# Joint and up projection of an encoder layer: sum tiles of the last token tile, a third raw-weight place, and the order of passes and Gelu behind the evictions

## The chip, the cores and the metric

The kernel runs on one core of a Trainium2 chip. The metric is the device time of one execution in microseconds. Five engines work side by side, each through its own queue in order: TensorE (PE: matmuls and transposes), VectorE (DVE), ScalarE (ACT), GpSimd (POOL), and SyncE (SP), which here only issues DMA transfers. An instruction starts when it is at the head of its queue and the semaphores it waits for have come.

## The reference

One layer of a post-norm encoder over 1024 tokens of width 1024, in float32. Three sub-layers, each `h = layer_norm(alpha*h + f(h))`: a token mixer (mLSTM and neighbourhood attention), cross-attention into 256 memory tokens, and a gated feed-forward part. What follows concerns the border between the second and the third, and the third's first half:

```
def conv_ffn(x, w_up, b_up, w_dw, b_dw, w_down, b_down):
    h = x @ w_up + b_up
    h = lax.conv_general_dilated(h, w_dw[:, None, :], ...width 3, depthwise...) + b_dw
    g, u = jnp.split(h, 2, axis=-1)
    y = jax.nn.gelu(g, approximate=False) * u
    return y @ w_down + b_down
```

The hidden width is 2816, so `w_up` has 5632 columns: 22 blocks of 128 gate columns and 22 of 128 up columns.

## The kernel before

**Numbers.** A float32 operand is held as two float16 parts, a high part and the rest. A product of two such operands is three matmuls (`mm3`, L224 to L226: high by high, high by rest, rest by high). A split takes one ACT pass for the high part (L203) and one DVE pass for the rest (L204). Weights are first scaled by a power of two found from their largest absolute value.

**Units.** The up projection is done in 22 units (`Units`, L1507), one for each block of gate columns with its block of up columns. A unit is a 2 by 2 block product done with seven products in place of eight: A11·B11, A12·B21, S1·T1, S2·T2, S3·T3, S4·B22 and A22·T4. A is the unit's weight, B the tokens; S1 to S4 are sums of weight blocks, T1 to T4 sums of token blocks. Each product is 4 slices times 3 matmuls of 128 by 512, so a unit has 84 matmuls.

A unit `v` goes through these stages:

- `load` (L1515): one DMA of 1 MB into a raw place. Units 0 and 1 use `two0` and `two1`; later ones rotate over the two places of the tile `ur`.
- `bound` (L1522): ACT takes absolute values and their sum over the raw tile (L1524), DVE casts the result to `am` (L1525).
- `scale` (L1530): PE turns `am` round through a small matmul (`mx`, L182), DVE makes the scale `us` from it (L183, L174 to L176, L1533).
- `sums` (L1543): POOL makes S1 to S4 from the raw tile (L1547 to L1550) into two places called `wraw`.
- `split_A` and `split_S`: ACT L203 and DVE L204, three pieces each, into the home of `v % 4` (`unitYh`, `unitA` with `whi` and `wlo`, `unitYl`, or `whi` and `wlo`). The first piece reads the raw tile, the other two the sums.
- the seven products, into three PSUM banks X, Z and W.
- `take` (L1706): the evictions. On ACT are `m1` (L1709, after A11·B11), `u2` (L1713, after S2·T2), `u3` (L1715, after S3·T3) and `C21` (L1719, after A22·T4). On DVE are `C11` (L1711), `C22` (L1717) and `C12` (L1721).
- `post` (L1685 and around): the convolution of width 3 for gate and up part (ACT L1683, DVE L1684 and L1685 each), then Gelu on ACT (L1689), a multiply on DVE (L1690), the store of `y` (L1691) and a pass of absolute values on ACT (L1692).

The unit loop also holds a survey of the down weights (`survey_down`): a 512 KB load into `sv0` or `sv1`, and a pass of absolute values on ACT (L1728).

**The joint.** Token tiles come out of cross-attention one by one (`out_d`: residual, L1480, then the layer norm, L237 to L252). `to_B` (L1377) transposes a tile on PE (tile `tp`, L1381), evicts it with weight and bias of the norm (ACT L1284 for six of eight slices, DVE L1286 for two), and, for tiles with an odd number, makes T1 to T4 (DVE L1414, L1415, L1418, L1422) and splits them and B22 (`pair`: ACT L1411, DVE L1412). The sums T1 to T4 of a tile stand in the units' `wraw` places, except for the last two tiles: the last but one, here r6, uses `ysum`, and the last, r7, uses three tiles called `spare`, which share the places `vec0`, `vec1`, `vec2` with the surveys' `sv0` and `sv1`. Units 0 and 1 have their A11·B11 and A12·B21 beside this, and wait with S1·T1 for r7's T1.

**Who sets the order.** The program is written in the order of the listing, but the order in which each engine issues is set by a scheduler of the language, which lays the instructions out on a timeline of its own; `tc.issue_after(x)` makes an instruction stand behind `x` in the issue order. A tile's place is taken again when all readers of the one before are done (`reuse_waits="tile"`).

## Time and profile before

| what | value |
|---|---|
| three timed runs | 1477.83, 1480.55 and 1480.89 us, median 1480.55 us |
| the profiled execution, time | 1481.55 us |
| its span in the profile | 1479.8 us |
| mean granted TensorE clock | 0.993 |
| PE busy | 1435.1 us (97%) |
| DVE busy | 1034.1 us (70%) |
| ACT busy | 821.5 us (56%) |
| POOL busy | 553.5 us (37%) |

Times in the trace count from the start of the span. The profiled execution's own time is 1.75 us more than its span. The joint lies at about 820 to 850 us, the unit loop ends at about 1200 us, and behind it come the down projection and the last norm. Groups of instructions are named by engine and line; a row of a timeline gives the start, the duration, the engine, the line, output and inputs, and in brackets how long the engine stood idle before it and what ended that.

### The profile page before, as it was taken

The page shows a single profiled execution, that of the slowest core. Times are in us where ns is not written, and L with a number is a line of the kernel's source. Part 1 is how long each engine was busy: PE and PEld are TensorE (multiplying, and loading weights), DVE is VectorE, ACT ScalarE, POOL GpSimd, SP SyncE. Part 2 cuts the span into 40 slices and gives each one's busy share as a digit, 9 for nine tenths or more (in the row PEclk, how much of TensorE's full clock was granted, in tenths as well). Part 3 has the DMA queues.
Part 4 walks back from the last instruction along what each step waited for, and adds up shares of the span by engine and source line. Part 5 has one row for each costly group of instructions (what it writes and reads, how often), then busy time and mean ns, then how long its engine had stood idle before and what let it go on. Part 6 is the DMA issues. An engine that isn't in the chain of part 4 may idle for free. (4 is left out here: it accounts for less than half of the span.)

```text
span 1479.8 us, 21506 instructions
## 1 busy us (share of the span) xinstructions
PE 1435.1 (97%) x7996; PEld 844.2 (57%) x7996; DVE 1034.1 (70%) x1950; ACT 821.5 (56%) x1385; POOL 553.5 (37%) x440
## 2 busy tenths in 40 slices
PE   8999899999999999999999899999999999999998
PEld 6998776456766777774444444444444444444445
DVE  7867866535777778589658878787888888707424
ACT  5765465565563576424455777777777767403001
POOL 4452356502334766055114153343444400300543
PEclk9999999999999999999999999999999999999999
DMA  8845654214654644643343333233322437603121
GB/s 302 318 180 198 184 190 153 84 50 129 159 147 152 206 142 141 256 148 72 86 100 86 116 143 128 114 114 128 114 114 113 144 142 242 228 28 110 47 71 58
DMA packets 116383, 208.61 MB, mean 141 GB/s; under 512 B 40627, under 2 KB 69555, under 8 KB 112950
## 3 DMA queue, kind: packets, MB, share of 16 engines
q1 hardware_dynamic: 115984, 206.47, 42.0%
q8 instruction: 63, 1.03, 0.3%
q0 software_dynamic: 144, 0.49, 0.2%
q14 instruction: 42, 0.34, 0.1%
q10 hardware_dynamic: 150, 0.27, 0.0%
HBM read 154.15 MB, written 45.15 MB: 135 GB/s over the span
## 5 line engine op out<-in xcount | busy, mean ns | idle before, releaser
L1547 POOL TENSOR_TENSOR wraw<-ur 128x512 f32<-128x512 f32 x20 | 42.5, 2125 | 213.6 <-issue 193.0
L225 PE MATMUL dn<-wlo,yp 128*128 128x512 f16 (+1 forms) x284 | 105.1, 370 | 0.0
L224 PE MATMUL dn<-whi,yp 128*128 128x512 f16 (+1 forms) x284 | 104.9, 370 | 0.0
L226 PE MATMUL dn<-whi,yp 128*128 128x512 f16 (+1 forms) x284 | 104.4, 370 | 0.0
L1684 DVE SCALAR_TENSOR_TENSOR cbuf<-C,wdw,cbuf 128x1024 f32<-128x1024 f32 x44 | 71.4, 1623 | 30.8 <-ACT cbuf L1683 30.4
L225 PEld LDWEIGHTS <-whi 128*128 128x128 f16 x540 | 52.8, 98 | 58.0 <-issue 5.9
L226 PEld LDWEIGHTS <-wlo 128*128 128x128 f16 x540 | 52.8, 98 | 56.7 <-DVE wlo L204 1.3
L224 PEld LDWEIGHTS <-whi 128*128 128x128 f16 x540 | 52.8, 98 | 54.7 <-issue 1.7
L204 DVE SCALAR_TENSOR_TENSOR wlo<-wraw,us,whi 128x1024 f16<-128x1024 f32 (+1 forms) x48 | 62.8, 1325 | 21.3 <-ACT whi L203 21.3
L242 POOL TENSOR_TENSOR lnrs<-lnrs,mhalf 128x1 f32<-128x1 f32 x32 | 23.5, 735 | 127.4 <-DVE lnrs L241 90.2
L1685 DVE SCALAR_TENSOR_TENSOR cbuf<-C,wdw,cbuf 128x1024 f32<-128x1024 f32 x44 | 69.8, 1587 | 1.1
L1683 ACT ACTIVATE cbuf<-C,bdw,wdw 128x1024 f32<-128x1024 f32 x44 | 54.4, 1235 | 17.8 <-DVE C L1721 17.2
L1524 ACT ACTIVATE junk<-ur 128x2048 bf16<-128x2048 f32 x20 | 38.2, 1912 | 40.1 <-DMA ur<-in_w_up_dram 40.1
L203 ACT ACTIVATE whi<-wraw,us 128x1024 f16<-128x1024 f32 (+1 forms) x48 | 51.1, 1102 | 16.0 <-DVE us L176 15.8
L225 PEld LDWEIGHTS <-yp 128*128 128x128 f16 x370 | 36.2, 98 | 39.9
L224 PEld LDWEIGHTS <-yp 128*128 128x128 f16 x370 | 36.2, 98 | 39.8
L226 PEld LDWEIGHTS <-yp 128*128 128x128 f16 x370 | 36.2, 98 | 39.7
L224 PE MATMUL tk<-whi,Bo 128*128 128x256 f16 (+1 forms) x192 | 52.6, 274 | 2.9 <-DVE stage L204 2.9
L224 PE MATMUL tk<-whi,Be 128*128 128x256 f16 (+1 forms) x192 | 52.6, 274 | 0.9 <-DVE stage L204 0.8
L225 PE MATMUL tk<-wlo,Be 128*128 128x256 f16 (+1 forms) x192 | 52.4, 274 | 0.8 <-DVE wlo L204 0.8
L226 PE MATMUL tk<-whi,Bo 128*128 128x256 f16 (+1 forms) x192 | 52.5, 274 | 0.0
L226 PE MATMUL tk<-whi,Be 128*128 128x256 f16 (+1 forms) x192 | 52.5, 274 | 0.0
(555 smaller groups left out, 4802.2 us busy)
## 6 DMA issues: line engine op xcount, KB each, us to landing
ur<-in_w_up_dram SPq DMA_DIRECT2D x20, 1024.0 KB
sv<-in_w_down_dram SPq DMA_DIRECT2D x22, 512.0 KB
y<-cbuf SPq DMA_DIRECT2D x22, 512.0 KB
ur<-y SPq DMA_DIRECT2D x11, 1024.0 KB
wraw<-in_w_down_dram SPq DMA_DIRECT2D x22, 512.0 KB
r<-h SPq DMA_DIRECT2D x11, 512.0 KB
wraw<-in_w_tok_dram SPq DMA_DIRECT2D x10, 512.0 KB
wr<-in_w_xk_dram SPq DMA_DIRECT2D x8, 512.0 KB
```

Source lines behind the costliest of these rows:

```text
L203: A.activation(hi, src, AF.Copy, scale=s)
L204: return V.scalar_tensor_tensor(lo, src, s, hi, op0=OP.mult, op1=OP.subtract)
L224: T.matmul(ps, lh, rh, start=first, stop=False, skip_group_check=skip)
L225: T.matmul(ps, lh, rl, start=False, stop=False, skip_group_check=skip)
L226: return T.matmul(ps, ll, rh, start=False, stop=last, skip_group_check=skip)
L242: G.tensor_tensor(rs[:, 0:1], rs[:, 0:1], mhalf[:, 0:1], OP.pow)
L1524: A.activation(junk, self.raw[v], AF.Abs, accum_out=l1)
L1547: G.tensor_tensor(S1, A21, A22, OP.add)
L1683: A.activation(c, C[:, 1:SEQ + 1], AF.Identity, scale=wdw[:, 1, j:j + 1], bias=bdw[:, j:j + 1])
L1684: V.scalar_tensor_tensor(c, C[:, 0:SEQ], wdw[:, 0, j:j + 1], c, op0=OP.mult, op1=OP.add)
L1685: V.scalar_tensor_tensor(c, C[:, 2:SEQ + 2], wdw[:, 2, j:j + 1], c, op0=OP.mult, op1=OP.add)
```

## The change

Line numbers of the new kernel are 6 to 11 higher in this region: L1709 becomes L1717, L1689 becomes L1697, L1524 becomes L1531, L1480 becomes L1490, L1412 becomes L1420.

1. A new pool, `raws`, holds `two0` and `two1` to the end of the kernel, and `raw8()` gives out three places in turn: `two0`, `two1` and one `ur` (which had two places). Unit loads, the `y` tiles of the down projection (`y_pair`) and some of its weights (`w_pair`) take their place there.
2. The last tile's sums T1 to T4 go to the `wraw` places, like those of the earlier tiles; `spare` 0 and 2 are gone, `spare` 1 stays.
3. `to_B` of r6 is written between the two halves of r7's output product, where it stood behind them.
4. Unit 2's `bound` stands behind r7's T3 pair, and every later `bound(v+3)` behind the eviction `u2` of unit `v`.
5. The second half of `post` (Gelu, multiply, store, absolute pass) is kept in `ending` and issued in the next unit, behind that unit's `m1`.

```diff
+        rt2 = cb_.enter_context(tc.tile_pool(name="raws", bufs=1, side="right", reuse_waits="tile"))
+        raws = [0]
+
+        def raw8(shape=[128, 2 * D]):
+            i = raws[0] % 3
+            raws[0] += 1
+            return rt2.tile(shape, F32, name=f"two{i}") if i < 2 else pools["ur"].tile(shape, F32, name="ur")
...
-            t12, t34 = ((spare(2 * i) if tt == todo[-1] else yl[:, i * 1024:i * 1024 + 1024] if tt == todo[-2] else
+            t12, t34 = ((yl[:, i * 1024:i * 1024 + 1024] if tt == todo[-2] else
                          wp.tile([128, WP], F32, name="wraw", tag="wraw", bufs=2)[:, :1024]).rearrange(
...
-            pair("T3", T3)
+            ends = pair("T3", T3)
...
+            return ends
...
-                if v < 2:
-                    self.raw[v] = rt.tile([128, 2 * D], F32, name=f"two{v}")
-                elif v < NFF:
-                    self.raw[v] = pools["ur"].tile([128, 2048], F32, name="ur", tag="ur", bufs=2)
                 if v < NFF:
+                    self.raw[v] = raw8()
                     return S.dma_start(self.raw[v], I["w_up"][v])
...
         run(o6)
         next(o7)
+        to_B(*rq.pop(0))
         next(o7)
         with tc.issue_after(stores[-1].ins):
             units.load(2)
         run(o7)
-        to_B(*rq.pop(0))
...
-                    to_B(*rq.pop(0))
+                    ends = to_B(*rq.pop(0))
...
-            units.bound(2, junk)
+            with tc.issue_after(ends[0].ins), tc.issue_after(ends[1].ins):
+                units.bound(2, junk)
...
-                raw = ur.tile([128, 2048], F32, name="ur", tag="ur", bufs=2)
+                raw = raw8()
...
-                    t = f16(ur.tile([128, 2048], F32, name="ur", tag="ur", bufs=2))
+                    t = f16(raw8())
...
-            loaded, posts = None, []
+            loaded, posts, ending = None, [], ()
...
                 if v > 1:
-                    take(v, "m1")
+                    first = take(v, "m1")
+                    with tc.issue_after(first.ins):
+                        run(ending)
...
-                take(v, "u2")
+                second = take(v, "u2")
...
-                units.bound(v + 3, junk)
+                with tc.issue_after(second.ins):
+                    units.bound(v + 3, junk)
...
-                if posts:
-                    run(posts.pop())
+                ending = posts.pop() if posts else ()
...
             v = NFF - 1
+            run(ending)
```

**Where the order moves: ACT in the unit loop.** ACT's rows of the kernel before, from the eviction `u2` of unit 13 (`C2`) to the first split piece of unit 16 (`unitYh`). `junk` is the bound of unit 17, `sv` a survey, `cbuf` the convolution of unit 12 (L1683 its first pass, L1689 the Gelu, L1692 the absolute pass), `C3` the `u3` of unit 13 and `C4` the `m1` of unit 14.

```order
L1713 ACTIVATE C2_9044<-z_10697,bup_7149,us_10449 128x4x128
L1524 ACTIVATE junk_8639,l1_10903<-ur_10821 128x2048
L1728 ACTIVATE sv0_9040,sums_92<-sv0_9040 128x1024
L1683 ACTIVATE cbuf_9039<-C0_9042,bdw_9061,wdw_9060 128x1024
L1715 ACTIVATE C3_9045<-z_10697,bup_7149,us_10449 128x4x128
L1689 ACTIVATE cbuf_9039<-cbuf_9039 128x1024
L1709 ACTIVATE C4_9046<-z_10829,bup_7149,us_10581 128x4x128
L1692 ACTIVATE cbuf_9039,sums_92<-cbuf_9039 128x1024
L203 ACTIVATE unitYh_8670<-ur_10689,us_10845 128x1536
```

The same stretch of ACT's queue in the changed kernel:

```order
L1721 ACTIVATE C2_9047<-z_10696,bup_7152,us_10452 128x4x128
L1531 ACTIVATE junk_8642,l1_10774<-two1_10688 128x2048
L1736 ACTIVATE sv1_9044,sums_92<-sv1_9044 128x1024
L1691 ACTIVATE cbuf_9042<-C0_9045,bdw_9064,wdw_9063 128x1024
L1723 ACTIVATE C3_9048<-z_10696,bup_7152,us_10452 128x4x128
L1717 ACTIVATE C4_9049<-z_10828,bup_7152,us_10584 128x4x128
L1697 ACTIVATE cbuf_9042<-cbuf_9042 128x1024
L203 ACTIVATE unitYh_8673<-two1_10688,us_10848 128x1536
L203 ACTIVATE unitYh_8673<-wraw_10822,us_10848 128x1024
L203 ACTIVATE unitYh_8673<-wraw_10823,us_10848 128x1024
L1700 ACTIVATE cbuf_9042,sums_92<-cbuf_9042 128x1024
```

The Gelu has moved from ahead of `m1` of unit 14 to behind it, the absolute pass from ahead of the splits to behind them, and the bound behind this `u2` is that of unit 16, whose split follows in the same stretch, where it was that of unit 17.

**DVE in the joint.** DVE's rows of the kernel before, from r7's first residual to r7's layer norm (L244); `ysum` is where r6's sums T1 to T4 stand.

```order
L1480 SCALAR_TENSOR_TENSOR r7_7426<-r7_7426,sc_94,S2_8840 128x512
L237 BN_STATS lnst_8894<-r7_7426 128x6
L204 SCALAR_TENSOR_TENSOR wlo_8778<-wraw_8736,us_8768,whi_8777 128x1024
L204 SCALAR_TENSOR_TENSOR wlo_8778<-wraw_8737,us_8768,whi_8777 128x1024
L1480 SCALAR_TENSOR_TENSOR r7_7426<-r7_7426,sc_94,S2_8866 128x512
L237 BN_STATS lnst_8894<-r7_7426 128x6
L239 BN_AGGR lnmv_8897<-lnst_8894 128x2
L1525 CAST am_9030<-l1_9031 128x1
L241 TENSOR_SCALAR lnrs_8899<-lnmv_8897,sc_94 128x1
L1414 TENSOR_TENSOR ysum_8922<-r6_7384,Bf_7509 128x512
L1286 TENSOR_SCALAR r6_7384<-tp_8909,wb2_7147 128x128 x2
L244 TENSOR_SCALAR r7_7426<-r7_7426,lnmv_8897,lnrs_8899 128x1024
```

The same stretch in the changed kernel, from the splits of unit 1 on; L244 of r7 stands three rows behind its last row.

```order
L204 SCALAR_TENSOR_TENSOR wlo_8781<-wraw_8740,us_8771,whi_8780 128x1024
L1423 TENSOR_TENSOR ysum_8887<-r6_7387,Bf_7512 128x512
L1490 SCALAR_TENSOR_TENSOR r7_7429<-r7_7429,sc_94,S2_8902 128x512
L1286 TENSOR_SCALAR r6_7387<-tp_8874,wb2_7150 128x128 x2
L237 BN_STATS lnst_8930<-r7_7429 128x6
L1420 TENSOR_TENSOR TX1l_8341<-ysum_8887,TX1l_8341 128x4x128
L1424 TENSOR_TENSOR ysum_8887<-r6_7387,ysum_8887 128x512
L1427 TENSOR_TENSOR ysum_8887<-r6_7387 128x512
L239 BN_AGGR lnmv_8933<-lnst_8930 128x2
L1420 TENSOR_TENSOR wlo_7530<-r6_7387,whi_7529 128x4x128
L1431 TENSOR_TENSOR ysum_8887<-Bf_7512,ysum_8887 128x512
L241 TENSOR_SCALAR lnrs_8935<-lnmv_8933,sc_94 128x1
```

Work on r6 (L1423, L1286, L1420, L1424, L1427, L1431) now stands ahead of r7's second residual (L1490) and between it and r7's norm, where it followed that norm.

**ACT behind the joint.** ACT's rows of the changed kernel from the T3 pair of r7 on; `unitYl` is unit 2's home, and the last row is the eviction `u2` of unit 0.

```order
L1419 ACTIVATE TX1l_8341<-wraw_8989 128x4x128
L1531 ACTIVATE junk_8642,l1_9034<-ur_8928 128x2048
L1419 ACTIVATE TX1h_8340<-wraw_8989 128x4x128
L1736 ACTIVATE sv1_9044,sums_92<-sv1_9044 128x1024
L1736 ACTIVATE sv1_9044,sums_92<-sv1_9044 128x1024
L203 ACTIVATE unitYl_9084<-ur_8928,us_9076 128x1536
L203 ACTIVATE unitYl_9084<-wraw_9070,us_9076 128x1024
L203 ACTIVATE unitYl_9084<-wraw_9071,us_9076 128x1024
L1721 ACTIVATE C0_9045<-z_8940,bup_7152,us_8545 128x4x128
```

Unit 2's bound, which stood ahead of r6's pairs, now stands among r7's. Two surveys and unit 2's three split pieces stand ahead of the first `u2`; before, unit 2's three pieces, the first piece of unit 3 and two surveys stood there, in that order.

More of the change, by code (lines that the diff above doesn't have):

```diff
@@ L1321, in home @@
                 if n % 2 == 0:
-                    two[n // 2] = rt.tile([128, 2 * D], F32, name=f"two{n // 2}")
+                    two[n // 2] = rt2.tile([128, 2 * D], F32, name=f"two{n // 2}")
                 rs[n] = two[n // 2][:, n % 2 * D:n % 2 * D + D]
@@ L1410, in pair @@
                 h, l = (t[:, :, o] for t in Bop[n])
-                A.activation(h, src, AF.Copy)
-                (G if n in ("B22", "T3") and tt not in todo[-2:] else V).tensor_tensor(l, src, h, OP.subtract)
+                a = A.activation(h, src, AF.Copy)
+                b = (G if n in ("B22", "T3") and tt not in todo[-2:] else V).tensor_tensor(l, src, h, OP.subtract)
+                return a, b
             V.tensor_tensor(T1, e12, B1[:, 0], OP.subtract)
@@ L1708, in take @@
                 if what == "m1":
-                    A.activation(g0, j4(X[v]), AF.Identity, scale=c, bias=bg)
+                    return A.activation(g0, j4(X[v]), AF.Identity, scale=c, bias=bg)
                 elif what == "C11":
@@ L1712, in take @@
                 elif what == "u2":
-                    A.activation(g1, j4(X[v]), AF.Identity, scale=c, bias=bg)
+                    return A.activation(g1, j4(X[v]), AF.Identity, scale=c, bias=bg)
                 elif what == "u3":
```

## Prediction

> **What bounds the kernel now.** I read the windows first, to find where TensorE (PE) is not busy; then its waits, to see who ends them; then the timeline of one unit and the chain of waits, to see why. The windows, with the columns length, then busy time and count of PE, PEld, DVE, ACT and POOL, the granted clock, and the share and rate of DMA:
>
> ```profile
> 800.00:850.00 50.00, 45.37 (x220) 21.82 (x219) 42.07 (x81) 34.93 (x58) 13.68 (x23) 0.97 0.31 101
> 850.00:1200.00 350.00, 343.78 (x1595) 155.14 (x1594) 277.71 (x317) 262.12 (x305) 143.89 (x76) 1.00 0.33 122
> 1200.00:1450.00 250.00, 250.00 (x1163) 113.90 (x1161) 138.78 (x163) 77.61 (x78) 54.71 (x26) 1.00 0.36 124
> ```
>
> PE is the bound. It is idle for 4.6 us in the joint and 6.2 us in the 350 us of the unit loop, and never in the 250 us behind. So the change can win only what lies in the first two rows. PE's waits, first from 850 to 1200 us and then from 835 to 850 us, with the time in all, the count and the longest:
>
> ```profile
> PE z L224 <- ACT C L1709: 3.3, 8, 0.9
> PE z L224 <- ACT C L1713: 1.6, 3, 0.8
> PE z L224 <- ACT C L1715: 0.9, 2, 0.6
> PE mx L182 <- DVE am L1525: 0.4, 1, 0.4
> ```
>
> ```profile
> PE mx L182 <- DVE us L183: 1.5, 1, 1.5
> PE mx L182 <- ACT spare L1284: 1.0, 1, 1.0
> PE z L224 <- ACT TX1h L1411: 0.8, 1, 0.8
> PE z L225 <- DVE TX1l L1412: 0.6, 1, 0.6
> PE z L224 <- ACT TX1l L1411: 0.6, 1, 0.6
> ```
>
> The first list sums to the 6.2 us of the window, in 14 waits, and nearly all of them are for an eviction on ACT (m1, u2, u3). One such wait in the timeline:
>
> ```profile
> 1090.33 1.91 ACT L1524 ACTIVATE junk<-ur 128x2048 bf16<-128x2048 f32 x1 [2.32 <-DMA ur<-in_w_up_dram]
> 1094.54 1.28 DVE L1684 SCALAR_TENSOR_TENSOR cbuf<-C,wdw,cbuf 128x1024 f32<-128x1024 f32 x1 [1.36 <-ACT cbuf L1683]
> 1094.83 0.38 PE L225 MATMUL z<-Bh,unitYl 128*128 128x512 f16 x1
> 1097.17 1.06 ACT L1689 ACTIVATE cbuf<-cbuf 128x1024 f32<-128x1024 f32 x1 [2.00 <-DVE cbuf L1685]
> 1097.86 0.38 PE L226 MATMUL z<-TX1h,unitA 128*128 128x512 f16 x1
> 1098.14 0.77 ACT L1709 ACTIVATE C<-z,bup,us 128x512 f32<-128x512 f32 x1
> 1098.95 0.38 PE L224 MATMUL z<-TX1h,unitYl 128*128 128x512 f16 x1 [0.51 <-ACT C L1709]
> ```
>
> From 1094.83 to 1097.86 PE starts 14 matmuls, 0.216 us apart, although a row gives 0.38: the last matmul ahead of a gap hides 0.16 us of it. So 14 waits are worth 6.2 + 14 x 0.16 = 8.4 us, and the joint's five 4.5 + 5 x 0.16 = 5.3 us. The wait itself: the product S2·T2 needs m1, m1 stands behind the Gelu, and the Gelu waits 2.00 us for the convolution on DVE. The convolution is late because ACT stood 2.32 us at the bound, waiting for a load. Why the load is late, the chain of waits says:
>
> ```profile
> 1104.07 5.06 DMA ur<-in_w_up_dram
> ...
> 1109.15 1.27 ACT junk L1524
> ...
> 1118.37 1.15 ACT cbuf L1692 x2
> 1119.52 1.47 ACT unitA L203
> ...
> 1121.02 1.83 DVE unitA L204
> ...
> 1122.90 4.79 DMA ur<-in_w_up_dram
> ```
>
> It is a ring: with two raw places a load starts when the split of an earlier unit has read its place, the bound waits for that load, the convolution for the bound, the multiply, the pass and the next split for the convolution. One turn takes 18.83 us (1104.07 to 1122.90); PE's 84 matmuls at 0.216 and the small mx are 18.2.
>
> **The change, part by part.**
>
> *Third raw place and bound behind u2.* A load has a whole unit more, over 18 us, for a transfer of 5.06. The DMA leaves the ring, and with it the 2.32 us that ACT stands there. The bound now queues behind u2 of unit v, for which ACT waits on PE: behind it are a survey, the gate part's first pass, u3 and the next m1. The bound takes 1.91, its sum 0.19, then the cast on DVE; mx is due 10.3 us after the end of S2·T2 (S1·T1, S4·B22, S3·T3 and A11·B11, 48 matmuls). The cast comes about 4.5 us after that end (u2 0.77, bound and sum, and behind two passes of the convolution on DVE), so this wait hides with over 5 us to spare. Without that cover every us too late is paid once per unit.
>
> *Gelu, multiply, store, pass behind the next m1.* m1 then ends 0.85 us after A11·B11, and S2·T2 begins 5.2 us after it (24 matmuls of A12·B21 and A22·T4): 4.3 us of slack where the rows show a lack of 0.5. The waits for u2 and u3 go with it, as both stood behind the same bound. What is moved costs nothing on PE; on ACT the splits now stand ahead of the pass L1692 (1.15 here), which nothing on PE waits for, and SP's store of y waits for the multiply some 2 us longer, with only loads behind it that have a unit to spare.
>
> *What is late next* is the round of DVE and ACT by themselves. DVE is busy 277.71 of 350 us, or 14.8 us for a unit of 18.7; added to it are the waits on ACT that the order keeps: 1.36 ahead of L1684 and about 1.5 for the first split piece (L203, 1.47). That is 17.7, 0.5 below PE's 18.2. So PE is the bound, by a little, and I take the loop at -8.4 us; if the round came to 18.5, 18 units would lag by 0.3 each, 5.4 in all, of which the 4.3 of slack hide all but 1.1.
>
> *Joint.* r6's transposes stand inside r7's output product, and r6's sums and pairs ahead of r7's norm on DVE. Two rows of DVE, r7's second residual at the end of that product and r7's norm:
>
> ```profile
> 826.32 0.75 DVE L1480 SCALAR_TENSOR_TENSOR r<-r,sc,S 128x512 f32<-128x512 f32 x1 [0.23 <-PE S L226]
> 833.67 2.04 DVE L244 TENSOR_SCALAR r<-r,lnmv,lnrs 128x1024 f32<-128x1024 f32 x1
> ```
>
> PE ends that product near 826.3, now with eight transposes more inside, so near 827; 48 matmuls of A11·B11 and A12·B21 follow, 10.4 us, and r7's transposes stand at 837.4. The residual now waits for r6's evictions, until about 828; between it and the norm are nine operations of r6 and r7 of 0.6 to 0.7 us and two small ones: 834.5, or 836.5 with a norm of 2.04. So this hides, with 0.9 us to spare; an eviction of r6 that comes later than that delays the joint by as much. On SP the loads of units 3 and 4 now stand ahead of stores of h that are read only behind the loop. From r7's transposes on the path is as before:
>
> ```profile
> 838.13 2.19 ACT L1284 ACTIVATE spare<-tp,wb 128x128 f32<-128x128 f32 x6
> 840.19 1.48 ACT L1709 ACTIVATE C<-z,bup,us 128x512 f32<-128x512 f32 x2
> 841.52 0.66 ACT L1411 ACTIVATE TX1l<-spare 128x512 f16<-128x512 f32 x1
> 844.18 0.68 DVE L1412 TENSOR_TENSOR TX1l<-spare,TX1l 128x512 f16<-128x512 f32 x1
> 844.91 0.58 PE L225 MATMUL z<-TX1l,unitYh 128*128 128x512 f16 x1 [0.65 <-DVE TX1l L1412]
> ```
>
> Evictions, two m1, the high part of T1, its rest on DVE, then S1·T1. The high part is out at 842.18, its rest only starts at 844.18: DVE has sums, C11 and the scales of units 2 and 3 ahead of it. The scales are gone from there in the changed order, the sums and C11 are not. The gain lies between 0 and these 2.0 us; I take 0.86, so that the rest of T1 ends at 844.0 where it ended at 844.86. The clock takes half of that back:
>
> ```profile
> 839.00:840.00 1.00, 0.22 (x1) 0.10 (x1) 1.00 (x3) 1.00 (x4) 0.00 (x0) 1.00 0.07 15
> 844.00:845.00 1.00, 0.35 (x2) 0.09 (x1) 1.00 (x3) 0.14 (x1) 0.00 (x0) 0.50 0.00 0
> 848.00:849.00 1.00, 1.00 (x6) 0.47 (x5) 1.00 (x4) 1.00 (x2) 0.00 (x0) 1.00 0.88 254
> ```
>
> After the idle stretch the granted clock is 0.5 and comes back by 848. PE is as idle there as before, so I keep the half clock to the same moment: 0.86 us more of work at half speed loses 0.43, and 0.43 is left. [...]
>
> Against this stands unit 2. Its bound is now behind r7's T3 pair, and its sums on POOL wait for r7's pairs to leave the sum places. Its split pieces stand ahead of u2 of unit 0:
>
> ```profile
> 846.16 1.58 ACT L203 ACTIVATE unitYl<-ur,us 128x1536 f16<-128x1536 f32 x1
> 847.64 2.17 ACT L203 ACTIVATE unitYl<-wraw,us 128x1024 f16<-128x1024 f32 x2
> ```
>
> mx of unit 2 comes after 23 matmuls of S1·T1 and S2·T2, eight of them at half clock: 850.7. The scale takes 1.2 (my estimate: five small DVE operations in a row), the splits 3.7, u2 0.77: 856.4. PE has by then 23 more matmuls, to 855.7, and waits 0.7 (bounds 0 and 2, by whether the surveys ahead of the splits still wait for their load). The joint comes to -0.43 + 0.7 = +0.3; its bounds are -2.5 and +2, with r7's norm in the upper one.
>
> *Behind the loop* nothing changes on PE: three places where there were two for the y tiles, and one Gelu moved by 2 us under the down projection, where PE has no wait at all. I take nothing.
>
> *Sum.* -8.4 + 0.3 = -8.1 us, on the profiled execution 1481.55 - 8.1 = 1473.4. The median of the timed runs lies 1.0 below that execution, so the forecast is 1472.4 us.
>
> **The rivals.**
>
> *The wait only moves* (0.19). DVE and ACT set the round: in place of 17.7 it takes 18.6 to 18.8, today's turn, as the margin of 0.5 is a sum of means. For it speaks that ACT waits for DVE and DVE for ACT several times a unit; against it, that both have idle time and their loops are tied to PE only at m1. Then 18 units lag by 0.4 to 0.6 each, and less the 4.3 of slack 2.9 to 6.5 of the 8.4 us are given back: 1475.3 to 1478.9.
>
> *The joint gives more* (0.12). The rest of T1 comes the full 2.0 us earlier, or the clock is not halved (in before four us at 0.5 cost some 1.2, since PE was idle in part of them), and u2 of unit 0 is in time. Then the joint is worth -2.5 and the time 1469.6.
>
> *Slower, by the sums on POOL* (0.07). Place: the gate part's convolution. It runs just after the sums:
>
> ```profile
> 1031.51 2.29 DVE L1684 SCALAR_TENSOR_TENSOR cbuf<-C,wdw,cbuf 128x1024 f32<-128x1024 f32 x1
> 1037.23 1.27 POOL L1550 TENSOR_TENSOR wraw<-ur,wraw 128x512 f32<-128x512 f32 x1
> 1038.51 1.28 DVE L1684 SCALAR_TENSOR_TENSOR cbuf<-C,wdw,cbuf 128x1024 f32<-128x1024 f32 x1 [1.36 <-ACT cbuf L1683]
> ```
>
> The up part's pass beside POOL takes 2.29, the gate part's alone 1.28, and POOL ends at 1038.50, at the very start of that pass. If the removed waits pull the gate part forward under the sums, each of its two passes costs 1.0 more. With both, DVE's round is 19.7, 1.5 over PE, in 18 units 27 us less 4.3 of slack: 1495. One pass alone, 18.7 a round, gives back 4.7 of the gain; slower than before by 3 us it is from 1.4 us of overlap a unit on. [...]
>
> *The change does nothing measurable* (0.06): another load or a bank release keeps the ring at 18.8. Nothing in the rows shows one; the order shows the moves are made. Then 1480.
>
> **How the numbers follow.** My forecast has 0.56. A difference of 0.2%, 3 us, is about what can be told from no change. Faster by more than that, below 1477.6: 0.56 + 0.12 + 0.12 of the first rival = 0.80; within: 0.07 of the first rival and 0.05 of the last = 0.12; slower: 0.07 of the third and 0.01 of the last = 0.08. The range runs from 1468, the joint's best case, to 1479, the first rival's end.
>
> **What would show it.** In the profile after: PE over 349 us busy in the loop's 350; no idle time of ACT at L1531 for a load; no wait for L1717; mx 18.2 us apart. The joint is right if PE's first long run of S1·T1 starts near 844, the clock is back by 848, and one wait for L1721 stands near 856. It is wrong if mx stays 18.5 or more apart, if the new L1692 takes over 2 us twice a unit, or if PE waits for L244 ahead of r7's transposes.

## The result and the profile after

| what | before | changed |
|---|---|---|
| median of 14 timed runs | 1480.35 us | 1476.29 us |
| lowest and highest | 1476.70 and 1483.62 us | 1473.20 and 1479.50 us |
| ratio, 95% interval | | 0.9977 (0.9966 to 0.9987) |
| the profiled execution, its span | 1481.55, 1479.8 us | 1474.43, 1472.4 us |

The changed kernel is faster by about 3.4 us (1.9 to 5.0). The forecast was a gain of 8.1. The two profiled executions are further apart, by 7.4 us of span, so the first thing to settle is where those lie. The matmul `mx` runs once in each unit; its rows for units 1, 8 and 21, of the kernel before and then of the changed one:

```profile
810.73 0.22 PE L182 MATMUL mx<-identb,am 128*128 128x128 bf16 x1
943.76 0.22 PE L182 MATMUL mx<-identb,am 128*128 128x128 bf16 x1
1186.62 0.22 PE L182 MATMUL mx<-identb,am 128*128 128x128 bf16 x1
```

```profile
807.70 0.22 PE L182 MATMUL mx<-identb,am 128*128 128x128 bf16 x1
942.77 0.22 PE L182 MATMUL mx<-identb,am 128*128 128x128 bf16 x1
1179.19 0.22 PE L182 MATMUL mx<-identb,am 128*128 128x128 bf16 x1
```

They cut the execution into four parts. Up to unit 1's mx the changed profile is 3.0 us ahead, although PE issues the same instructions in the same order there: that is one execution against another, not the change (over the fourteen profiles of this study the mx of unit 0 starts anywhere from 783.6 to 788.2 us). From unit 1 to unit 8, the **joint stretch**, it takes 135.1 where it took 133.0: 2.0 us lost. From unit 8 to unit 21, the **loop stretch**, 236.4 where it was 242.9: 6.4 won. Behind it, 293.2 in both. So the change is worth -4.4 us in these two profiles, within the interval of the timed runs, and from here on kernels are compared by these two stretches, which leave the rest of the execution out. One thing still moves the joint stretch between executions: behind the idle time of PE at the joint the granted clock reads 0.50 for a while, 3.4 us in both of these profiles, none or 6.8 in some of the others. The last section prices it, and the table below gives it for each kernel.

The windows of the changed kernel, with the same columns as before:

```profile
800.00:850.00 50.00, 45.53 (x221) 22.16 (x220) 36.51 (x70) 29.45 (x53) 13.07 (x22) 0.97 0.42 136
850.00:1200.00 350.00, 345.96 (x1615) 156.81 (x1613) 281.82 (x327) 268.46 (x307) 148.59 (x76) 1.00 0.32 121
1200.00:1450.00 250.00, 250.00 (x1163) 113.88 (x1162) 135.26 (x165) 76.59 (x78) 59.05 (x28) 1.00 0.34 120
```

PE is idle for 4.0 us in the second row, not under 1 as forecast. Its waits, from 800 to 850 and then from 850 to 1200 us:

```profile
PE z L224 <- ACT TX1l L1419: 3.7, 1, 3.7
PE z L224 <- ACT TX1h L1419: 0.4, 1, 0.4
PE z L225 <- DVE TX1l L1420: 0.3, 1, 0.3
```

```profile
PE z L224 <- ACT unitYl L203: 2.2, 1, 2.2
PE z L224 <- ACT C L1721: 1.3, 2, 1.1
PE z L224 <- ACT C L1723: 0.3, 1, 0.3
```

The waits for m1 (L1709 before) are gone. What is new is one wait of 2.2 us for unit 2's split, one of 1.1 for the first u2, and one of 3.7 for the high part of r7's T1. ACT's timeline names the cause of the first two; `sv` is a survey of the down weights, `unitYl` unit 2's split, L1721 the u2 of unit 0:

```profile
842.32 0.65 ACT L1419 ACTIVATE TX1h<-wraw 128x512 f16<-128x512 f32 x1
845.57 1.06 ACT L1736 ACTIVATE sv<-sv 128x1024 f32<-128x1024 f32 x1 [2.60 <-DMA sv<-in_w_down_dram]
...
850.71 1.06 ACT L1736 ACTIVATE sv<-sv 128x1024 f32<-128x1024 f32 x1 [3.99 <-DMA sv<-in_w_down_dram]
...
851.77 1.56 ACT L203 ACTIVATE unitYl<-ur,us 128x1536 f16<-128x1536 f32 x1
853.23 2.17 ACT L203 ACTIVATE unitYl<-wraw,us 128x1024 f16<-128x1024 f32 x2
855.32 0.76 ACT L1721 ACTIVATE C<-z,bup,us 128x512 f32<-128x512 f32 x1
```

Both surveys use the same place, `sv1`. The first pass ends at 846.63, the second load is issued at 846.75, and ACT stands 3.99 us ahead of the second pass. The scale of unit 2 was there long before: its last DVE step begins at 848.45 and takes 0.20, and the split starts at 851.77. In the loop, a turn of ACT now reads:

```profile
1088.46 0.78 ACT L1717 ACTIVATE C<-z,bup,us 128x512 f32<-128x512 f32 x1 [1.59 <-PE z L226]
1089.14 1.04 ACT L1697 ACTIVATE cbuf<-cbuf 128x1024 f32<-128x1024 f32 x1
1090.09 1.56 ACT L203 ACTIVATE unitYh<-two,us 128x1536 f16<-128x1536 f32 x1
1091.55 2.17 ACT L203 ACTIVATE unitYh<-wraw,us 128x1024 f16<-128x1024 f32 x2
1093.63 1.04 ACT L1700 ACTIVATE cbuf<-cbuf 128x1024 f32<-128x1024 f32 x1
```

m1 waits for PE, 1.59 us, not PE for m1. The Gelu (L1697) finds its convolution done, and the absolute pass (L1700) comes behind the splits. From unit 9 to unit 21 mx follows mx by 18.19 us, PE's own 84 matmuls, 0.216 us apart.

### The profile page after: what moved, and what is told of

The parts are those of the page before. It is cut to its first block, busy times and chain, and to the rows that moved or that the text cites. A ratio compares the mean times of both kernels' runs of the same rounds, so it can differ in the third digit from the quotient of the medians.

```text
span 1472.4 us, 21481 instructions
## 1 busy us (share of the span) xinstructions
PE 1432.3 (97%) x7996; PEld 844.1 (57%) x7996; DVE 1027.0 (70%) x1950; ACT 822.2 (56%) x1385; POOL 559.4 (38%) x440
## 4 chain that ended last, share of the span: by engine, by line
PE 77%; DVE 9%; DMA 5%; ACT 4%; issue 2%; POOL 1%; SPq 0%; DVEq 0%; ACTq 0%; POOLq 0%
PE z L224 7%; PE z L226 7%; PE z L225 7%; PE dn L224 5%; PE dn L226 5%; PE dn L225 5%; PE S L224 4%; PE S L225 4%; PE S L226 4%; DVE wlo L204 2%; PE cl L224 2%; PE cl L225 2%; PE cl L226 2%; PE cu L226 1%; PE tk L225 1%
## 5 line engine op out<-in xcount | busy, mean ns | idle before, releaser
L1692 DVE SCALAR_TENSOR_TENSOR cbuf<-C,wdw,cbuf 128x1024 f32<-128x1024 f32 x44 | 66.2, 1506 | 34.0 <-ACT cbuf L1691 34.0
L1554 POOL TENSOR_TENSOR wraw<-two 128x512 f32<-128x512 f32 x15 | 31.1, 2071 | 126.7 <-issue 126.7
L1693 DVE SCALAR_TENSOR_TENSOR cbuf<-C,wdw,cbuf 128x1024 f32<-128x1024 f32 x44 | 71.8, 1632 | 1.1
L1691 ACT ACTIVATE cbuf<-C,bdw,wdw 128x1024 f32<-128x1024 f32 x44 | 54.5, 1238 | 21.0 <-DVE C L1729 20.3
L252 ACT ACTIVATE r<-r,lnrs 128x1024 f32<-128x1024 f32 x11 | 13.6, 1236 | 79.0 <-DVE lnrs L251 78.9
L224 PE MATMUL tk<-whi,Be 128*128 128x256 f16 (+1 forms) x192 | 52.6, 274 | 0.4 <-DVE stage L204 0.4
L225 PE MATMUL tk<-wlo,Bo 128*128 128x256 f16 (+1 forms) x192 | 52.5, 274 | 0.0
```

Of the source, the lines that this page charges most:

```text
L224: T.matmul(ps, lh, rh, start=first, stop=False, skip_group_check=skip)
L225: T.matmul(ps, lh, rl, start=False, stop=False, skip_group_check=skip)
L252: A.activation(r, r, AF.Identity, scale=rs[:, 0:1], bias=rs[:, 1:2])
L1554: G.tensor_tensor(S1, A21, A22, OP.add)
L1691: A.activation(c, C[:, 1:SEQ + 1], AF.Identity, scale=wdw[:, 1, j:j + 1], bias=bdw[:, j:j + 1])
L1692: V.scalar_tensor_tensor(c, C[:, 0:SEQ], wdw[:, 0, j:j + 1], c, op0=OP.mult, op1=OP.add)
```

## The experiments

Columns: the ratio to the kernel before with its 95% interval; then from each profile the joint stretch, the loop stretch, the usual turn in it (from mx to mx), and the time at half clock in the joint, all in us.

| kernel | ratio | joint | loop | turn | half clock |
|---|---|---|---|---|---|
| before | 1 | 133.0 | 242.9 | 18.57 to 18.85 | 3.4 |
| changed | 0.9977 (0.9966 to 0.9987) | 135.1 | 236.4 | 18.19 | 3.4 |
| changed, one survey later | 0.9950 (0.9938 to 0.9963) | 132.6 | 236.4 | 18.19 | 6.8 |
| before, one survey later | 1.0010 (1.0000 to 1.0020) | 132.5 | 243.3 | 18.56 to 18.92 | 6.8 |
| changed, two raw places | 0.9966 (0.9953 to 0.9980) | 134.2 | 237.0 | 18.19 | 6.8 |
| changed, Gelu unmoved | 1.0046 (1.0029 to 1.0063) | 136.3 | 244.0 | 18.57 | 6.8 |
| before, Gelu behind m1 | 0.9966 (0.9952 to 0.9979) | 134.6 | 236.4 | 18.19 | 3.4 |
| survey later, pass ahead of split | 1.0007 (0.9996 to 1.0017) | 131.1 | 244.7 | 18.70 | 3.4 |
| survey later, r6 behind | 0.9912 (0.9896 to 0.9929) | 128.0 | 236.4 | 18.19 | 0 |
| survey later, held matmuls | 0.9935 (0.9921 to 0.9948) | 130.3 | 236.4 | 18.19 | 3.4 |
| r6 behind, spare sums | 0.9943 (0.9921 to 0.9965) | 132.1 | 236.4 | 18.19 | 3.4 |
| r6 behind, two raw places | 0.9943 (0.9927 to 0.9960) | 131.5 | 237.0 | 18.19 | 3.4 |
| r6 behind, bound unmoved | 0.9926 (0.9907 to 0.9945) | 129.6 | 236.4 | 18.19 | 0 |
| changed, only r6 behind | 0.9959 (0.9944 to 0.9974) | 132.8 | 236.4 | 18.19 | 3.4 |

### One survey later, in the changed kernel and in the one before

Theory: the second survey's load costs the joint what the forecast missed. Rival: unit 2's own scale or sums are late. In both kernels the extra survey of unit 0 moves to unit 4.

```diff
-                    if v in (0, 10):
+                    if v in (4, 10):
                         survey_down(NFF - 1 - v // 10)
```

> The changed kernel with one of the two surveys that stand ahead of unit 2's split at the joint moved to unit 4. Theory A (the second survey's 512 KB transfer holds ACT for 3.99 us, and the split and u2 of unit 0 behind it): the split starts when the scale is ready, PE's two waits of 2.2 and 1.1 us near 855 shrink to under 0.8 us together, and the time falls by about 3 us, to some 0.998 of the changed kernel (0.9955 of the kernel before). Theory B (unit 2's own bound, mx, scale and sums are late): the waits stay above 2.5 us and the time stays within 0.5 us of the changed kernel.

> The kernel before with the same survey moved to unit 4. Theory A: no survey stood ahead of unit 2's split there, so nothing is gained: ratio 1.000 within 0.001. Theory C (a survey at the joint costs in any order, by its transfer or its pass): 1 us or more is gained, 0.999 or less.

Measured: 0.9950 and 1.0010. ACT of the changed kernel with the survey moved:

```profile
844.92 1.06 ACT L1736 ACTIVATE sv<-sv 128x1024 f32<-128x1024 f32 x1 [2.69 <-DMA sv<-in_w_down_dram]
...
848.48 1.58 ACT L203 ACTIVATE unitYl<-ur,us 128x1536 f16<-128x1536 f32 x1 [2.41 <-DVE us L176]
849.96 2.17 ACT L203 ACTIVATE unitYl<-wraw,us 128x1024 f16<-128x1024 f32 x2
852.04 0.76 ACT L1721 ACTIVATE C<-z,bup,us 128x512 f32<-128x512 f32 x1
```

The split now waits for its scale, and PE's waits from 835 to 860 us:

```profile
PE z L224 <- ACT TX1l L1419: 3.7, 1, 3.7
PE z L224 <- ACT C L1721: 0.3, 1, 0.3
```

The two waits of 3.3 us are down to 0.3. From unit 2's mx to unit 3's it takes 11.77 us where it took 14.97: 3.2 won there. The whole joint stretch is 2.5 shorter: from unit 1's mx to unit 2's, where this profile has 3.4 us more at half clock, it is 0.7 longer. The two ratios, 0.9977 and 0.9950, are 4.0 us apart. Theory A holds; theory B falls. In the kernel before, the same edit gains nothing in time: no survey stood ahead of that split, so C falls too.

### Two raw places, and Gelu where it was

The forecast put the loop's gain down to the third raw place. Rival: the order of Gelu and pass alone. One part of the change is undone in each kernel. In the first, the y tiles and weights of the down projection take their place in `ur2()` as well; in the second, `ending` and its `issue_after(first)` are removed and the second half of `post` runs where it ran before.

```diff
-                if v < NFF:
-                    self.raw[v] = raw8()
+                if v < 2:
+                    self.raw[v] = raw8()
+                elif v < NFF:
+                    self.raw[v] = ur2()
...
+        def ur2():
+            return pools["ur"].tile([128, 2 * D], F32, name="ur", tag="ur", bufs=2)
```

```diff
-                    with tc.issue_after(first.ins):
-                        run(ending)
...
-                ending = posts.pop() if posts else ()
+                if posts:
+                    run(posts.pop())
```

> The changed kernel with two raw places for units 2 and on, as before, all else as changed. Theory D (the third place is what frees the loop): one turn from mx to mx goes back to 18.5 to 18.85 us, ACT waits for the load at the bound again, PE waits 4 us or more in the loop. Theory E (the order of bound and Gelu is what frees it): the turn stays at 18.2 us and PE waits under 2 us in the loop.

> The changed kernel with Gelu, multiply, store and absolute pass where they were written before, all else as changed. Theory D: with loads a unit early the convolution is early too, the Gelu ahead of m1 no longer waits long, the turn stays within 0.05 of 18.2 us. Theory E: m1 stands behind the Gelu's wait for the convolution and the turn is 18.4 us or more, PE's waits for m1 come back in the loop with 2 us or more.

Measured: with two places the turn is 18.19 all the same; only the units up to 9 are slower, with turns up to 19.84 and four waits of PE, 3.3 us in all. With three places and the Gelu unmoved the usual turn is 18.57, and the kernel is slower than before. Theory D, which was the forecast's, is wrong. Theory E is right on the turn but not on PE's waits in the second kernel: those for m1 are 1.1 us, not 2 or more, and 4.6 are for u3 (L1723). A turn of ACT with the Gelu unmoved and three places:

```profile
1097.49 1.06 ACT L1697 ACTIVATE cbuf<-cbuf 128x1024 f32<-128x1024 f32 x1 [2.24 <-DVE cbuf L1693]
1098.45 0.77 ACT L1717 ACTIVATE C<-z,bup,us 128x512 f32<-128x512 f32 x1
1099.86 1.06 ACT L1700 ACTIVATE cbuf<-cbuf 128x1024 f32<-128x1024 f32 x1 [0.64 <-DVE cbuf L1698]
...
1100.91 1.56 ACT L203 ACTIVATE unitYh<-two,us 128x1536 f16<-128x1536 f32 x1
```

and DVE's rows of the same turn:

```profile
1098.61 1.22 DVE L1698 TENSOR_TENSOR cbuf<-cbuf 128x1024 f32<-128x1024 f32 x1
...
1102.50 1.82 DVE L204 SCALAR_TENSOR_TENSOR unitYh<-two,us,unitYh 128x1536 f16<-128x1536 f32 x1 [1.84 <-ACT unitYh L203]
```

The unit's load does not stand in it: ACT has no idle time at L1531 in this kernel. ACT does wait 1.43 us for a survey's load at 1110.48, but the convolution's pass behind that survey (L1691, 1111.89) then waits 0.26 more for DVE, so here that load does not set the turn either. What is left is DVE and ACT handing work to each other: convolution, Gelu, multiply, pass, split, next convolution. The pass waits 0.64 us for the multiply, takes 1.06 and then its sum, and the split stands behind it; DVE waits 1.84 for the split. In the changed order that wait of DVE is gone. This is theory F, and it got two tests.

### Gelu behind m1 alone, and the pass put back ahead of the split

The kernel before with part 5 alone (the lines of `first`, `ending` and `run(ending)` of the change, nothing else); and the changed kernel, survey moved, with the split's three pieces issued behind the pass:

```diff
-                A.activation(cu, cg, AF.Abs, accum_out=ysum[:, v:v + 1])
+                units.last = A.activation(cu, cg, AF.Abs, accum_out=ysum[:, v:v + 1])
...
+                with (tc.issue_after(self.last.ins) if self.last is not None else nullcontext()):
                     split16(ah, al, self.raw.pop(v)[:, 512:], self.s[v][0])
```

(The same `with` stands ahead of the two other pieces.)

> The kernel before with one part alone: Gelu, multiply, store and absolute pass behind the next unit's m1; two raw places, bound and joint as before. Theory F (the turn is set by DVE and ACT handing work to each other, and the absolute pass with its wait for the multiply stood in that ring ahead of the split): the turn falls from 18.6 to 18.85 to 18.2 us from unit 9 on, ACT's wait for the load at the bound falls with it, 5 to 6 us are gained, 0.996 to 0.997. Theory D (two raw places set the turn through the load): the turn stays 18.5 us or more and less than 2 us are gained.

> The changed kernel with the survey moved, and in the loop the three split pieces of a unit issued behind the absolute pass; the Gelu stays behind m1. Theory F: the pass and its wait are back in the ring of DVE and ACT, the free turn is 18.5 us; m1 is ahead of the Gelu, so PE waits only once the lag has used up 4 us of slack, and 1 to 3 us are lost against the kernel with the survey moved: 0.996 to 0.997. Theory G (only m1's place behind the Gelu mattered): turn 18.2 us, 0.995 as with the survey moved.

Measured: part 5 alone gives 0.9966 and the full loop stretch of 236.4. (Its joint is 1.6 us longer than before; behind 855 us PE waits 1.7 for the cast of a unit, L1525.) ACT still waits for the load at the bound in it, and it does not matter. The idle time of ACT ahead of L1524 from 945 to 1180 us, in the kernel before and then with part 5 alone (us in all, times):

```profile
  DMA ur<-in_w_up_dram: 24.3, 12
```

```profile
  DMA ur<-in_w_up_dram: 19.4, 12
```

Four fifths of the wait are still there, 1.6 us a unit, and the turn is PE's own. So the load's wait fills time that ACT has to spare in this order; the chain of waits named it because it ended last, not because the turn needed it shorter. I had expected it to shrink with the turn, which it did only a little.

With the pass ahead of the split the turn is 18.70 and the whole gain of the loop is lost, though m1 stands ahead of the Gelu: F holds and G falls. In this order the pass waits 3.30 us for the multiply (1097.90, L1703), where it waited 0.64 with the Gelu unmoved. So the run shows that the pass ahead of the split costs the gain; it does not show that the pass alone made the old turn of 18.57. The loss, 8.3 us in the loop stretch, is well above the 1 to 3 expected. I had let 4 us of slack absorb the lag; PE's waits from 855 us on show that there was none:

```profile
PE z L224 <- ACT C L1724: 3.3, 11, 0.4
PE z L224 <- ACT C L1726: 1.5, 2, 1.2
PE z L224 <- ACT C L1720: 1.1, 1, 1.1
```

L1724 is u2: PE waits for it in 11 of the turns. The slack I had counted is m1's. u2 stands behind the split on ACT, so it lags with the ring at once. The opposite order, Gelu ahead of m1 and the pass behind the split, was not tried, so how the loss of the old order divides between the two stays open.

### r6 behind r7's product, and held matmuls

This left the wait of 3.7 us for T1. PE of the changed kernel:

```profile
834.11 0.38 PE L226 MATMUL z<-Bh,unitA 128*128 128x512 f16 x1
834.32 1.04 PE L1389 MATMUL tp<-ident,r 128*128 128x128 f32 x8
839.07 0.38 PE L224 MATMUL z<-TX1l,unitYh 128*128 128x512 f16 x1 [3.71 <-ACT TX1l L1419]
```

r7's norm (L244) had ended at 832.31, two us before the transposes, and behind them PE has nothing left until T1. Theory H: the transposes come too late. Two kernels, both with the survey moved: one undoes part 3, which lets the scheduler put r7's transposes ahead of 16 matmuls of A12·B21; one keeps part 3 and holds the last six matmuls of unit 1's A12·B21 behind the transposes.

```diff
         next(o7)
-        to_B(*rq.pop(0))
         next(o7)
...
         run(o7)
+        to_B(*rq.pop(0))
```

```diff
-                prod(Z[v], v, "A12", "B21", True, True)
+                if v == 1:
+                    (ah, al), (bh, bl) = units.got[v]["A12"], Bop["B21"]
+                    for k in range(4):
+                        with (tc.issue_after(tp_last[0].ins) if k > 1 else nullcontext()):
+                            mm3(Z[v], ah[:, k, :], al[:, k, :], bh[:, k, :], bl[:, k, :], k == 0, k == 3, skip=True)
+                else:
+                    prod(Z[v], v, "A12", "B21", True, True)
```

(`tp_last` holds the transpose issued last, here of r7.)

> The changed kernel with the survey moved and the transposes and pairs of r6 written behind r7's output product again. r7's norm comes ahead of r6's pairs on DVE and r7's transposes come 11 matmuls earlier on PE. Theory H (at the joint PE waits for r7's own chain from its transposes on, and the changed order put the transposes too late): PE's wait of 3.7 us for the first S1.T1 shrinks by 1.5 to 2.4 us and the stretch from mx of unit 1 to mx of unit 8 (132.5 us with the survey moved) by 1 to 2 us. Theory I (r6's work is what holds the joint, so that its early place helps): the stretch grows by 1 us or more.

> The changed kernel with the survey moved and the last six matmuls of unit 1's A12.B21 held until r7's transposes are issued. Theory H: r7's norm was ready 1.7 us before PE came to its transposes, so all behind comes 1.3 us earlier, PE's wait for the first S1.T1 falls from 3.7 to 2.4 us, the stretch from mx of unit 1 to mx of unit 8 is 131.2 us: 0.994. Rival: the norm is not ready and PE waits for it, no gain.

Measured: joint stretch 128.0 and 130.3, ratios 0.9912 and 0.9935. PE with r6 behind:

```profile
833.63 1.04 PE L1389 MATMUL tp<-ident,r 128*128 128x128 f32 x8
...
838.37 0.38 PE L224 MATMUL z<-TX1l,unitYh 128*128 128x512 f16 x1 [0.25 <-ACT TX1l L1419]
```

The way from the transposes to T1 is as long as ever, 4.7 us, but PE works through 3.5 of it. The wait falls from 3.7 to 0.3. With six matmuls held it falls to 2.4, the 1.3 us expected, and the stretch by 2.2, more than the wait: this profile has 3.4 us at half clock, the one it is compared with 6.8. H holds; I falls. The version with r6 behind won 4.5 us of stretch where I expected 1 to 2: 16 matmuls stand behind the transposes, not 11, and no half clock is left (last section).

### What the other parts are worth, on the best version

Three kernels undo one more part each, on the version with r6 behind and the survey moved: the last tile's sums back in `spare`, two raw places, the loop's bound without its `issue_after`.

```diff
-            t12, t34 = ((yl[:, i * 1024:i * 1024 + 1024] if tt == todo[-2] else
+            t12, t34 = ((spare(2 * i) if tt == todo[-1] else yl[:, i * 1024:i * 1024 + 1024] if tt == todo[-2] else
```

```diff
-                with tc.issue_after(second.ins):
-                    units.bound(v + 3, junk)
+                units.bound(v + 3, junk)
```

> The best version so far (changed kernel, survey moved, r6 behind r7's product) with the last tile's sums back in the three spare tiles. Two surveys stand ahead of unit 2's split again, in different places. Theory J (the sum places as such do nothing for PE; what counts is what stands ahead of the split on ACT): the stretch from mx of unit 1 to mx of unit 8 grows from 128.0 only by what the surveys' loads hold up, 1 to 4 us, seen as a wait of ACT for a survey's load ahead of the split. Theory K (the sum places shorten r7's own chain): PE starts the long run of S1.T1 later as well, by 1 us or more after r7's transposes.

> The same best version with two raw places for units 2 and on. Theory L (the third place only helps the first units, where loads start late): turn 18.2 us from unit 9 on, the stretch from mx of unit 1 to mx of unit 8 is 1 to 3 us longer than 128.0, the time 0.1 to 0.2 per cent above the best version. Rival: the third place does nothing at all, stretch 128 within 0.5 us.

> The same best version with the bounds of the loop issued where the scheduler puts them, not behind u2. Theory L: turn 18.2 us in the loop all the same, since three places make loads early; at the joint two bounds (2.1 us each) stand ahead of unit 2's split or of the first evictions, which costs 0 to 2 us in the stretch to unit 8. Rival: bounds that run ahead hold evictions in the loop and the turn is 18.4 us or more.

Measured: joint stretches 132.1, 131.5 and 129.6, and 18.19 us a turn in all three.

The sums in `spare` also changed PE's order: only 4 matmuls are left behind r7's transposes, and a wait of 3.8 us is back. T1 comes 5.7 us behind the transposes where it came 4.7, which is K's sign; but the added time lies ahead of the sums, since ACT stands 3.03 us for r6's last sum (L1431) ahead of r7's evictions. So this run doesn't tell J from K; the scheduler's order moved with the edit.

With two places the stretch is 3.5 us longer than 128.0, above L's range, and the rival falls. Only 1.0 of it lies between unit 2's mx and unit 8's, where L looked for it (turns of 19.7 and 19.0 us, where three places give 18.6 and 18.9). The other 2.5 lie ahead of unit 2's mx: PE waits 1.6 for T1, and 3.4 us at half clock follow. ACT had stood 3.08 us for a survey's load (831.01) ahead of r6's pairs and r7's evictions; that load was issued at 822.25, behind two unit loads, where the best version issues it ahead of them. As far as the rows show, that part comes from a moved order of loads, not from a place that was missing in the units.

The bound's place is worth 1.6 us at the joint and nothing in the loop, as L had it.

### Only r6 behind

The changed kernel with part 3 alone undone, the surveys where the change has them (the diff of r6 above).

> The changed kernel with one part alone undone: r6's transposes and pairs behind r7's product, the two surveys ahead of unit 2's split as in the change. 16 matmuls then stand behind r7's transposes where none did. Theory M (the joint lost twice, by the survey's load and by the transposes' place, and the two add): PE's wait for the first S1.T1 is under 0.5 us as with both undone, the two waits for unit 2's split and the first u2 stay at 3 us or more together, the stretch from mx of unit 1 to mx of unit 8 is 131 us (135.1 with the change, 128.0 with both undone) and the ratio 0.993 to 0.995. Rival (one follows from the other): the stretch is 128 or 135.

Measured: 132.8 us, between the theory's 131 and the rival's 135, and 0.9959, above the theory's ratio. PE's waits from 800 to 855 us:

```profile
PE z L224 <- ACT unitYl L203: 3.3, 1, 3.3
PE z L225 <- DVE TX1l L1420: 0.5, 1, 0.5
PE z L224 <- ACT TX1h L1419: 0.4, 1, 0.4
PE z L224 <- ACT TX1l L1419: 0.3, 1, 0.3
```

The first u2 costs 1.1 more behind that. r6's place is repaired in full: from unit 1's mx to unit 2's it takes 35.84 us, as with both undone (35.83). From unit 2's mx to unit 3's it takes 16.59, where the changed kernel takes 14.97. The survey does not come later for it: from the first S1·T1 to the split's start it is 12.5 us here and 12.7 there. But PE does the matmuls between them at full clock, so it waits longer for the split, 3.3 where it was 2.2, and the half clock comes behind that wait, from 855.2 to 858.6. The half clock moved and did not go, which theory M had not counted; without the 1.5 us that such a stretch costs (last section), 131.3 is left, which is M's sum. Each repair alone wins 2.2 (r6) and 2.5 us (survey), both together 7.1. That is 2.3 more than the sum, about what the half clock accounts for: 3.4 us in the changed kernel and here, 6.8 with the survey alone moved, none with both.

## Why the prediction was right or wrong

**Where it was right.** PE is the bound and only the joint and the loop could give anything: behind the loop 293.2 us stand in both kernels. The loop stretch: 6.4 us won, all that PE had to win there, and a turn of 18.19 where 18.2 was written. (The forecast of -8.4 also counted the units ahead of that stretch; of them below.) Slower by the sums on POOL did not come about: in the turn from 1096 us the two L1692 take 1.69 and 1.28 us. r7's norm hides. The long run of S1·T1 starts at 841.17 in a profile that is 3.0 us ahead, so 844.2 in the time of the profile before, where 844.0 was forecast. The clock is back by 844, 847 in the time of the profile before (848 forecast), and there is a wait for L1721 near 856.

**The step that failed** is the sum of the joint, "-0.43 + 0.7 = +0.3". Its second term, unit 2's split and the first u2, was put at 0.7 with a bound of 2, "by whether the surveys ahead of the splits still wait for their load". They did, one after the other through one place; the two waits are 2.2 and 1.1 us, and with 0.16 hidden at each 3.6. Moving one survey took 3.0 of 3.3 us away. The bound should have been worked out: a place is taken again only when its reader is done (the second load was issued at 846.75, 0.12 us behind the end of the first pass), and the order rows showed two rows of `sv1` in a line. That one mis-sized term is 2.9 of the 3.7 us between the forecast of -8.1 and the -4.4 of the profiles. The rest is more than covered by four waits of PE of 0.2 to 0.5 us, 1.3 in all, in the units from 895 to 938 us, which I had let go to nothing; the other terms came out some 0.5 better than forecast.

**A step that was right for the wrong reason** is the loop. I took the ring to go through the load, because the chain of waits went through it, and gave the gain to the third place. The runs showed the ring in DVE and ACT; the place alone did nothing for the turn, part 5 alone did all, and with the pass put back ahead of the split the gain was gone. That the turn came out as written is luck in part. My sum of that round, 17.7, was for the new order, with waits taken from the old one: the 1.5 us that DVE waits for the first split piece are gone in the changed kernel. I made no such sum for the old order; the run with the Gelu unmoved shows what it had to give, 18.57 without any wait for the unit's load.

**A question not asked.** I checked that r7's norm comes in time for PE, and took that as harmless. It was 2.0 us early, and with all 48 matmuls ahead of the transposes nothing covered the 4.7 us behind them. This is no part of the error of the forecast, which had PE as idle there as before; it is a gain that was left lying. 16 matmuls behind the transposes are worth 4.5 us of stretch with the survey moved, half clock included, and 2.2 with the surveys as the change has them.

**The clock.** I kept the half clock of before, to the same moment, and the gain at T1 halved. That agreed here only by chance: three other profiles with the same wait of 3.7 us have 6.8 us of half clock where the changed kernel has 3.4 (last section).

## What to carry to other kernels

A wait that the chain shows is not yet a wait that counts: before giving a gain to a transfer, add up the round of the engines around it without the transfer. When a step moves, ask not only whether its input is ready but what the bound engine still has to do behind it, and let the engine reach a long chain of others with work in hand. Two loads through one place, queued ahead of a step on the path, cost most of the second load's time here: ACT stood 3.99 us, and PE lost 3.2. And before two single profiles are compared over a stretch, the time at half clock in each, here 0, 3.4 or 6.8 us, has to be put beside them.

## What the runs showed of the hardware that was not expected

The half clock at this joint came in pieces of 3.4 us: none, one or two of them in each of the fourteen profiles (the table's last column). Windows of four us at the joint, of the changed kernel, then with the survey moved, then with r6 behind; the granted clock is the third number from the right:

```profile
840.00:844.00 4.00, 3.58 (x10) 1.21 (x10) 3.98 (x7) 2.98 (x5) 1.54 (x1) 0.57 0.29 85
844.00:848.00 4.00, 4.00 (x21) 1.88 (x20) 0.89 (x2) 1.15 (x2) 3.92 (x4) 1.00 0.16 59
```

```profile
836.00:840.00 4.00, 1.66 (x4) 0.51 (x4) 3.96 (x8) 4.00 (x9) 0.00 (x0) 0.70 0.04 7
840.00:844.00 4.00, 3.94 (x10) 1.28 (x9) 3.83 (x6) 2.23 (x3) 2.21 (x2) 0.50 0.40 124
844.00:848.00 4.00, 4.00 (x19) 1.77 (x18) 0.37 (x2) 1.15 (x2) 3.43 (x3) 0.95 0.02 7
```

```profile
836.00:840.00 4.00, 3.30 (x14) 1.26 (x13) 3.96 (x8) 4.00 (x9) 0.00 (x0) 1.00 0.05 9
840.00:844.00 4.00, 3.53 (x17) 1.64 (x17) 3.87 (x6) 2.28 (x3) 2.17 (x2) 1.00 0.39 121
```

The first two have the same wait of 3.7 us and nearly the same instructions around it, yet half clock for 4 x 0.43 x 2 = 3.4 us in one and for (0.30 + 0.50 + 0.05) x 4 x 2 = 6.8 in the other: once and twice. In the third, whose waits there are 0.3, 0.4 and 0.5 us, there is none. The lengths are worked out from the shortfall to 1.00, against 0.50, the lowest clock of the rows at the joint: of before, the row from 844 to 845 us (prediction) reads 0.50, and so do the two behind it. Why the same wait has one such stretch with it in one execution and two in another, no run here shows.

What one stretch of 3.4 us costs, two profiles show: the changed kernel with the survey moved, and the same with the pass ahead of the split. Up to unit 8 their mx follow each other at the same distances to 0.03 us, but for one: from unit 1 to unit 2 it is 40.39 us in the first, with 6.8 us at half clock, and 38.91 in the second, with 3.4. That is 1.5 us for one stretch more, where half of 3.4 would be 1.7 (at half clock the changed kernel's matmuls start 0.43 us apart, from 841.55 to 842.83, where 0.216 is usual); PE waits in part of it.

A wait of 3.7 or 3.8 us for T1 came with one stretch in three profiles and with two in three. A shorter longest wait did not keep it away: 2.4 us (held matmuls) and 1.6 us (two places, r6 behind) came with one each, and the kernel before has one with five waits of 0.6 to 1.5 us in a row, 4.5 in all. For a forecast I would put, as an estimate from these profiles, 1.5 to 1.7 us for each stretch of half clock in which PE has work, and one or two of them behind a joint like this one.
